# Some lo parts by ScalarE and accumulating transfers, two sorted groups of matmul passes and a sum of weights by a transfer, where the mixer's and the up projection begin

## The chip, the cores and the metric

The kernel runs on one core of a Trainium2 chip. TensorE multiplies, VectorE and ScalarE do elementwise work, GpSimd here does little but issue transfers, SyncE issues most of the loads and stores. The metric is the device time of one execution, in microseconds (us), less is better; the reference's outputs are to be met in float32.

## The reference

One step of a layer with 512 prompt tokens and 8 sampled ones, in float32: a mixer (a short gated convolution and a gated linear attention side by side), then a gated convolutional feed-forward block.

```python
def mixer(xn, conv_prev, gla_prev, w_in, conv_w, gate_w2, gate_b, gla_norm_g, w_out, chunk):
    proj = xn @ w_in
    bg, cg, hin, q, k, v, og, glr = jnp.split(proj, [_S1, _S2, _S3, _S4, _S5, _S6, _S7], axis=-1)
    cu, conv_new = causal_dwconv(cg * hin, conv_prev, conv_w)
    ya = bg * cu
    ...
    out = jnp.concatenate([ya, yb], axis=-1) @ w_out
    return out, conv_new, s_new

def conv_ffn(xn, prev, w_up, conv_w, conv_b, w_down):
    u, v = jnp.split(xn @ w_up, 2, axis=-1)
    cu, new = causal_dwconv(u, prev, conv_w)
    h = jax.nn.silu(cu + conv_b) * v
    return h @ w_down, new

    # in trunk, for the one layer
        m, c_new, s_new = mixer(rmsnorm(x, norm_mix_g[l]), conv_prev[l], gla_prev[l], w_in[l],
                                conv_w[l], gate_w2[l], gate_b[l], gla_norm_g[l], w_out[l], chunk)
        x = x + m
        f, f_new = conv_ffn(rmsnorm(x, norm_ffn_g[l]), ffn_prev[l], w_up[l], ffn_conv_w[l],
                            ffn_conv_b[l], w_down[l])
        x = x + f
```

The model width is 2048, the feed-forward width 5632, so `w_up` has 11264 columns.

## The kernel before

**Three passes.** A float32 product is made of three matmuls in a rounded format. `split` (L121) writes `hi`, a rounded copy of a tile, by ScalarE (L123), and `lo = src - hi` by VectorE (L124); a product then adds w_hi·x_hi, w_lo·x_hi and w_hi·x_lo. Activations are held transposed, 128 channels by T = 520 tokens, and a matmul takes half of them, HT = 260.

**Seven products.** The large projections are cut into groups: 12 of the mixer's ("mix"), 2 × 4 of the output projection ("wo", two halves c of the contraction by four g of the columns), 44 of the up projection ("up"), then "down". Each group is a 2 × 2 block product made with seven products instead of eight, in the order 1, 5, 6, 2, 7, 3, 4, of 24 matmuls each. It needs sums of weights (`s` and one `raw`, made by L1318 on VectorE, where the seventh product's sum `raw[2,1] + raw[1,1]` may be an accumulating transfer from GpSimd instead, L1322) and sums of activations, the forms f = 4 to 7. Forms 1, 2, 3 are the activations themselves. In the traces a tile of hi activations is called `yh`, its lo `yl`, or `bh` and `bl`, or `b` for both, where it lies in the memory of a residual tile `acc`.

**What sets the order.** The main loop runs over the products (`up_product`, `chunk_product`). While product i runs, `prepare(i + 2)` issues hi (L1373) and lo (L1377) of the weights two products ahead, and `run_steps` takes further work from generators which name the half product at which they go on. The order of the instructions on TensorE, VectorE, ScalarE and GpSimd is held as it was written; each engine works through its own queue in that order, so that a waiting instruction holds up all behind it.

**Where mix begins.** Ahead of its first group stands a projection (L140). `begin(0)` loads its weights; its seventh sum is VectorE's. `load_sum` (L1749) loads a sum of activations from DRAM into the lo tile, and returns a `split` to be called later; `put_sums` (L1851) calls those of the forms 6 and 7 while the first group runs. `R2` is the square of the normalizing factor R.

**Where up begins.** During the second half of wo (c = 1), `projected(g)` (L1682) takes each finished quarter q of the residual, `acc[g, q]`. `ready` stores it (`x_d<-acc`) and scales it into a tile `t`; `square` squares it into `fh` by ScalarE and adds that onto `ssq` or `R` by an accumulating transfer (L1706). `split` makes the forms 1, 2, 3, and `out` either splits the sums or, for g < 3, stores them in DRAM (`t_d`), to be loaded back as `yl` and split by `split_sums`; form 7 is split at once for every g. Form 2 and 3's tiles lie in the memory of `acc` tiles, so that they can be written only when the store of that quarter has read it. The first product of up waits for the last of all this, that of g = 3.

Of the kernel before, what the change touches and what calls it, by code (L numbers as in the profile page):

```python
# [9 lines left out]
F32 = mybir.dt.float32  # L10
F32R = mybir.dt.float32r
U8 = mybir.dt.uint8
AF = mybir.ActivationFunctionType
ALU = mybir.AluOpType
# [23 lines left out]
def trunk_kernel(  # L38
# [6 lines left out]
    nc = tc.nc  # L45
# [75 lines left out]
    def split(src, hi, lo, scale=None):  # L121
        if scale is None:
            nc.scalar.activation(hi, src, AF.Copy)  # L123
            nc.vector.tensor_tensor(lo, src, hi.bitcast(F32), op=ALU.subtract)  # L124
        else:
            nc.scalar.activation(hi, src, AF.Copy, scale=scale)
            nc.vector.scalar_tensor_tensor(
                lo, src, scale, hi.bitcast(F32), op0=ALU.mult, op1=ALU.subtract
            )

    def halves(t):
        return t[:, :HT], t[:, HT:T]
# [44 lines left out]
    def span(ps, w, acts, k0, pk0, nk, nkt):  # L177

        outs = [x[:, :HT] for x in ps]
        for k in range(k0, k0 + nk):  # L180
            mm3(outs, (w[0][:, k - pk0, :], w[1][:, k - pk0, :]), acts[k], k == 0, k == nkt - 1)
# [93 lines left out]
    mt_d = dp.tile([4, 4, P, T], F32, name="mt_d")  # L275
# [475 lines left out]
    xq, homes = {}, {}  # L751
# [539 lines left out]
    def source(kind, at):  # L1291
        if kind == "mix":
            return lambda m, k: mix_source(*at, m, k)
        if kind == "up":
            return lambda m, k: up_source(*at, m, k)
        return lambda m, k: chunk_source(kind, w_out if kind == "wo" else w_down, *at, m, k)
# [50 lines left out]
    def begin(n):  # L1347
        kind, at = groups[n]

        state[kind, at] = weights(  # L1350
            source(kind, at), kind == "up" or kind in ("mix", "wo") and at[0] > 0,
            None if n else early,
        )

# [32 lines left out]
    def up_product(i):  # L1387
        kind, at, r = order[i]
        st = state[kind, at]
        b = BANK[r]  # L1390
        if b not in st["bank"]:
            st["bank"][b] = mm_bank()[:, :HT]
        wh, wl = (x.rearrange("p (k c) -> p k c", k=8) for x in (his.pop(i), los.pop(i)))
        for k in range(8):
            xh, xl = xq[INPUT[r], k]
            for j, (w, x) in enumerate(((wh, xh), (wl, xh), (wh, xl))):
                nc.tensor.matmul(  # L1397
                    st["bank"][b], w[:, k, :], x, start=b not in st["used"] and k == 0 and j == 0,
                    stop=k == 7 and j == 2, skip_group_check=True,
                )  # L1400
        st["used"].add(b)

    def copied(st, b):
# [36 lines left out]
    def mult(out, x, y):  # L1440
        nc.vector.tensor_tensor(out, x, y, op=ALU.mult)
# [240 lines left out]
    def projected(g):  # L1682
# [24 lines left out]

        def out(f, t):

            if f == 7 or g == NG - 1:  # L1710
                split(t, *form(f, g))
            else:
                nc.sync.dma_start(t_d[f - 4, g], t)

# [29 lines left out]
        square(2)  # L1744
        out(6, t3)
        yield 11
        split(xg[3], *form(3, g))

    def load_sum(d, f, g):  # L1749

        hi, lo = form(f, g)
        x = lo.bitcast(F32)
        nc.sync.dma_start(x, d[f - 4, g])
        return lambda: split(x, hi, lo)

    def split_sums():
# [63 lines left out]
    ps = new_mm()  # L1820
    w = next_half()
    prepare(0)
    span(ps, w, xa, 0, 0, 4, KD)
    for x in put[:3]:
        x()
# [5 lines left out]
        x()  # L1831
    evac(ps, y9)
    mult(y8, y8, on[0])
    mult(R2, R, R)
    bctx.close()
    yt3 = yctx.enter_context(tc.tile_pool(name="yt3", bufs=1))
    slots[12:] = [yt3] * 4
    put += [load_sum(mt_d, 7, g) for g in range(4)]
    for k in range(8):
        for f, kk, b in ((1, k, 0), (2, k + 8, 0), (3, k + 8, 1)):  # L1840
            xq[f, k] = [xa[kk][x][b] for x in range(2)]
# [7 lines left out]
        yield from leave(8, y8, y9)  # L1849

    def put_sums():  # L1851
        for x, n in zip(put[6:], (1, 1.5, 2, 3.5, 4, 4.5, 5)):
            yield n
            x()

# [252 lines left out]
```

## Time and profile before

| what | before |
|---|---|
| median of three runs | 2139.94 us (2136.82 to 2142.19) |
| the profiled execution | 2138.38 us |
| its span in the profile | 2136.7 us |
| granted TensorE clock | 0.997 |
| first product of mix, of up | about 376 us, 784 us |

The profile gives each engine's busy time. A view of waits names for an engine the line that waited, and what ended the wait; a row of the timeline gives start, duration, engine, line, operation, output <- inputs, and in brackets the idle time ahead of it with its releaser. Names there have no numbers: `R2 <- R` reads `R<-R`. "DVE" is VectorE, "ACT" ScalarE, "PE" TensorE, "POOL" GpSimd, "SP" SyncE. A row of the windows view has the stretch and its length, the busy time of PE, its weight loads, DVE, ACT and POOL with their instruction counts, the granted clock, the share of the 16 DMA engines, and GB/s.

### The profile page before, as it was taken

To read this page: it belongs to the slowest core of one execution; us is meant where nothing else is said; L and a number is where in the kernel's file an instruction comes from. 1 tells how busy PE (TensorE), PEld (TensorE's weight loads), DVE (VectorE), ACT (ScalarE), POOL (GpSimd) and SP (SyncE) were. 2 spreads that over 40 slices of the span, in tenths; PEclk is the share of its full clock that TensorE was granted. 3 is DMA by queue.
4 is the path that set the end of the run, shared out by engine and by line. 5 is a ranking of instruction groups with operands and counts; after the bars stand their busy time and mean duration, and the time that the engine had idled before them with its cause. 6 is when DMAs were issued, how large, how long until landed. Compare 5 with 4: busy or idle time off the path is not lost.

```text
span 2136.7 us, 44234 instructions
## 1 busy us (share of the span) xinstructions
PE 2109.9 (99%) x17880; PEld 2088.1 (98%) x17880; DVE 1763.6 (83%) x2349; ACT 1121.8 (53%) x1688; POOL 436.0 (20%) x623
## 2 busy tenths in 40 slices
PE   9999999999999999999999999999999999999997
PEld 8999989999999989999999999999999999999997
DVE  6556675988878898988988988988989778888886
ACT  7444543545544686555555555555555554444445
POOL 4212331112234211211311221212212200300000
PEclk9999999999999999999999999999999999999999
DMA  8455646877798996776776676776766875994734
GB/s 257 131 151 171 180 127 183 222 189 205 187 286 240 268 293 157 183 186 175 181 187 172 182 187 169 181 189 167 189 182 183 292 224 150 274 293 131 222 110 159
DMA packets 467757, 417.30 MB, mean 195 GB/s; under 512 B 21769, under 2 KB 426521, under 8 KB 467409
## 3 DMA queue, kind: packets, MB, share of 16 engines
q1 hardware_dynamic: 424209, 289.84, 47.8%
q0 software_dynamic: 43296, 124.57, 22.3%
q8 instruction: 140, 2.29, 0.5%
q14 instruction: 64, 0.52, 0.1%
q10 hardware_dynamic: 48, 0.07, 0.0%
HBM read 299.65 MB, written 80.31 MB: 178 GB/s over the span
## 4 chain that ended last, share of the span: by engine, by line
PE 62%; DMA 1%; DVE 1%; issue 1%; ACT 0%; POOL 0%; ACTq 0%; DVEq 0%; SPq 0%; POOLq 0%
PE mm L1397 29%; PE ms L1397 12%; PE x L1640 7%; PE y L1640 7%; PE f L1640 3%; PE e L1640 3%; PE mm L140 2%; DMA ssq<-fh 1%; DMA x_d<-acc 0%; PE ms L1998 0%; DMA yl<-t_d 0%; DVE yl L124 0%; DVE lo L1377 0%; DVE s L1318 0%; ACT y L2061 0%
## 5 line engine op out<-in xcount | busy, mean ns | idle before, releaser
L1397 PE MATMUL mm<-yl,hi 128*128 128x260 f32 x1792 | 504.1, 281 | 2.8 <-DVE yl L124 2.8
L1397 PE MATMUL mm<-yh,hi 128*128 128x260 f32 x1792 | 502.5, 280 | 0.6 <-DVE t L701 0.6
L1397 PE MATMUL mm<-yh,lo 128*128 128x260 f32 x1792 | 502.0, 280 | 0.8 <-DVE lo L1377 0.8
L1373 ACT ACTIVATE hi<-raw 128x1024 fp32r<-128x1024 f32 x336 | 354.4, 1055 | 245.4 <-issue 89.3
L1377 DVE TENSOR_TENSOR lo<-raw,hi 128x1024 fp32r<-128x1024 f32 x336 | 410.2, 1221 | 44.6 <-ACT hi L1373 40.8
L1377 DVE TENSOR_TENSOR lo<-s,hi 128x1024 fp32r<-128x1024 f32 x252 | 309.4, 1228 | 131.3 <-ACT hi L1373 129.9
L1373 ACT ACTIVATE hi<-s 128x1024 fp32r<-128x1024 f32 x252 | 266.3, 1057 | 233.2 <-PE ms L1397 97.3
L1397 PEld LDWEIGHTS mm<-yl,hi 128*128 128x128 f32 x1792 | 336.6, 188 | 3.7 <-DVE yl L124 3.7
L1397 PEld LDWEIGHTS mm<-yh,lo 128*128 128x128 f32 x1792 | 337.8, 189 | 1.2 <-DVE lo L1377 1.2
L1397 PEld LDWEIGHTS mm<-yh,hi 128*128 128x128 f32 x1792 | 337.7, 188 | 0.8 <-issue 0.8
L1397 PE MATMUL ms<-b,hi 128*128 128x260 f32 x1408 | 264.9, 280 | 0.0
L1397 PEld LDWEIGHTS ms<-b,hi 128*128 128x128 f32 x1408 | 222.0, 188 | 0.0
L1640 PE MATMUL y<-form,hi 128*128 128x260 f32 x1120 | 211.6, 281 | 0.6 <-DVE acc L1659 0.6
L1640 PE MATMUL x<-form,hi 128*128 128x260 f32 x1120 | 211.7, 281 | 0.1
L1318 DVE TENSOR_TENSOR s<-s,raw 128x1024 f32<-128x1024 f32 x168 | 205.2, 1222 | 2.9
L1397 PE MATMUL ms<-b,lo 128*128 128x260 f32 x704 | 197.0, 280 | 0.0
L1640 PEld LDWEIGHTS y<-form,hi 128*128 128x128 f32 x1120 | 176.5, 188 | 0.9 <-ACT hi L1373 0.7
L1640 PEld LDWEIGHTS x<-form,hi 128*128 128x128 f32 x1120 | 176.5, 188 | 0.6 <-issue 0.4
L1640 PE MATMUL x<-form,lo 128*128 128x260 f32 x560 | 157.0, 280 | 0.1
L1640 PE MATMUL y<-form,lo 128*128 128x260 f32 x560 | 156.9, 280 | 0.1
L1397 PEld LDWEIGHTS ms<-b,lo 128*128 128x128 f32 x704 | 132.0, 187 | 0.0
L1397 PE MATMUL mm<-bh,hi 128*128 128x260 f32 x448 | 125.5, 280 | 1.0 <-DVE acc L1659 1.0
(402 smaller groups left out, 4847.3 us busy)
## 6 DMA issues: line engine op xcount, KB each, us to landing
raw<-in_w_up_dram SPq DMA_DIRECT2D x176, 512.0 KB, 4.7
raw<-in_w_down_dram SPq DMA_DIRECT2D x96, 512.0 KB, 7.3
raw<-in_w_in_dram SPq DMA_DIRECT2D x92, 512.0 KB, 5.0
form<-f_d SPq DMA_DIRECT2D x126, 260.0 KB, 6.0
raw<-raw POOLq DMA_DIRECT2D x59, 512.0 KB, 5.3
f_d<-t POOLq DMA_DIRECT2D x80, 260.0 KB, 5.5
raw<-in_w_out_dram SPq DMA_DIRECT2D x32, 512.0 KB, 10.8
form<-g_d POOLq DMA_DIRECT2D x42, 260.0 KB, 7.5
```

The source lines that it names most:

```text
L140: nc.tensor.matmul(o, w, xx, start=first and i == 0, stop=last and i == 2)
L1318: return lambda: nc.vector.tensor_tensor(out, x, y, op=ALU.add)
L1373: nc.scalar.activation(his[i], src, AF.Copy)
L1377: nc.vector.tensor_tensor(los[i], src, his[i].bitcast(F32), op=ALU.subtract)
L1397: nc.tensor.matmul(st["bank"][b], w[:, k, :], x, start=b not in st["used"] and k == 0 and j == 0, stop=k == 7 and j == 2, skip_group_check ...
L1640: nc.tensor.matmul(ps[:, m, :], w[:, k, m * P : (m + 1) * P], x, start=b not in st["used"] and k == 0 and j == 0, stop=k == 3 and j == 2, ...
```

## The change

1. A new `split_by_dma`: ScalarE writes hi and then lo = −hi, and GpSimd issues a transfer that adds the source onto lo in memory. VectorE has no part in it.
2. `projected(g)` uses it for g = 0, 1, 2 in place of `split` for the forms 7 and 3; g = 3 stays. `put_sums` uses it for form 7 of g = 0 and 1, where the source of the transfer is the sum in DRAM. Eight subtractions of 128x520 leave VectorE, eight copies come to ScalarE, eight transfers of 260 KB to GpSimd's queue.
3. The seventh sum of the first mix group is an accumulating transfer too, issued right after `prepare(0)`.
4. `up_product` sorts the passes of the first group of mix and of up: over all eight k, those with the weights' lo part come last in mix, those with the activations' lo part in up. In the other groups the order is the old one.
5. The square of R goes from VectorE to ScalarE, and four of the times of `put_sums` come earlier.

```diff
--- before.py
+++ after.py
@@ -127,6 +127,12 @@
             nc.vector.scalar_tensor_tensor(
                 lo, src, scale, hi.bitcast(F32), op0=ALU.mult, op1=ALU.subtract
             )
+
+    def split_by_dma(src, hi, lo, again=None):
+        nc.scalar.activation(hi, src, AF.Copy)
+        nc.scalar.activation(lo, hi.bitcast(F32), AF.Copy, scale=-1.0)
+        again = src if again is None else again
+        nc.gpsimd.dma_start(lo.bitcast(F32), again, accum_op=ALU.add)
 
     def halves(t):
         return t[:, :HT], t[:, HT:T]
@@ -1348,7 +1354,7 @@
         kind, at = groups[n]
 
         state[kind, at] = weights(
-            source(kind, at), kind == "up" or kind in ("mix", "wo") and at[0] > 0,
+            source(kind, at), kind in ("mix", "up") or kind == "wo" and at[0] > 0,
             None if n else early,
         )
 
@@ -1391,13 +1397,16 @@
         if b not in st["bank"]:
             st["bank"][b] = mm_bank()[:, :HT]
         wh, wl = (x.rearrange("p (k c) -> p k c", k=8) for x in (his.pop(i), los.pop(i)))
-        for k in range(8):
-            xh, xl = xq[INPUT[r], k]
-            for j, (w, x) in enumerate(((wh, xh), (wl, xh), (wh, xl))):
-                nc.tensor.matmul(
-                    st["bank"][b], w[:, k, :], x, start=b not in st["used"] and k == 0 and j == 0,
-                    stop=k == 7 and j == 2, skip_group_check=True,
-                )
+        passes = [(k, j) for k in range(8) for j in range(3)]
+        if at == (0,):
+            late = 2 if kind == "up" else 1
+            passes.sort(key=lambda p: p[1] == late)
+        for k, j in passes:
+            x, w = xq[INPUT[r], k][j == 2], (wh, wl, wh)[j]
+            nc.tensor.matmul(
+                st["bank"][b], w[:, k, :], x, start=b not in st["used"] and (k, j) == (0, 0),
+                stop=(k, j) == (7, 2), skip_group_check=True,
+            )
         st["used"].add(b)
 
     def copied(st, b):
@@ -1707,8 +1716,10 @@
 
         def out(f, t):
 
-            if f == 7 or g == NG - 1:
+            if g == NG - 1:
                 split(t, *form(f, g))
+            elif f == 7:
+                split_by_dma(t, *form(f, g))
             else:
                 nc.sync.dma_start(t_d[f - 4, g], t)
 
@@ -1744,13 +1755,15 @@
         square(2)
         out(6, t3)
         yield 11
-        split(xg[3], *form(3, g))
-
-    def load_sum(d, f, g):
+        (split if g == NG - 1 else split_by_dma)(xg[3], *form(3, g))
+
+    def load_sum(d, f, g, by_dma=False):
 
         hi, lo = form(f, g)
         x = lo.bitcast(F32)
         nc.sync.dma_start(x, d[f - 4, g])
+        if by_dma:
+            return lambda: split_by_dma(x, hi, lo, d[f - 4, g])
         return lambda: split(x, hi, lo)
 
     def split_sums():
@@ -1820,6 +1833,7 @@
     ps = new_mm()
     w = next_half()
     prepare(0)
+    state[groups[0]]["seventh"]()
     span(ps, w, xa, 0, 0, 4, KD)
     for x in put[:3]:
         x()
@@ -1831,11 +1845,11 @@
         x()
     evac(ps, y9)
     mult(y8, y8, on[0])
-    mult(R2, R, R)
+    nc.scalar.activation(R2, R, AF.Square)
     bctx.close()
     yt3 = yctx.enter_context(tc.tile_pool(name="yt3", bufs=1))
     slots[12:] = [yt3] * 4
-    put += [load_sum(mt_d, 7, g) for g in range(4)]
+    put += [load_sum(mt_d, 7, g, g < 2) for g in range(4)]
     for k in range(8):
         for f, kk, b in ((1, k, 0), (2, k + 8, 0), (3, k + 8, 1)):
             xq[f, k] = [xa[kk][x][b] for x in range(2)]
@@ -1849,7 +1863,7 @@
         yield from leave(8, y8, y9)
 
     def put_sums():
-        for x, n in zip(put[6:], (1, 1.5, 2, 3.5, 4, 4.5, 5)):
+        for x, n in zip(put[6:], (1, 1.5, 2, 2.5, 3, 4, 4.5)):
             yield n
             x()
 
```

In the queues this reads as follows; the line numbers are those of each kernel's own file, so that L124's subtraction and the copies keep theirs while L1377 becomes L1383. VectorE, in the second half of the first mix group, from a lo part of `s` on (`t` and `zpad` are tiles of the mixer's gate):

```order
L1377 TENSOR_TENSOR lo_4977<-s_4663,hi_4975 128x1024
L124 TENSOR_TENSOR yl12_4821<-yl12_4821,yh12_4820 128x520
L704 TENSOR_TENSOR t_5007<-zpad0_854 128x260
L698 SCALAR_TENSOR_TENSOR t_5007<-t_5007,t_4688 128x260
L704 TENSOR_TENSOR t_5008<-t_4688,zpad0_854 128x260
L698 SCALAR_TENSOR_TENSOR t_5008<-t_5007,t_4688 128x260
L124 TENSOR_TENSOR yl13_4824<-yl13_4824,yh13_4823 128x520
L1377 TENSOR_TENSOR lo_5017<-raw_4534,hi_5015 128x1024
L124 TENSOR_TENSOR zpad0_854<-zpad0_854,fh_5019 128x260
L124 TENSOR_TENSOR yl14_4827<-yl14_4827,yh14_4826 128x520
L701 TENSOR_TENSOR t_5026<-mm_4840,t_4914 128x260
L124 TENSOR_TENSOR yl15_4830<-yl15_4830,yh15_4829 128x520
```

and now:

```order
L1383 TENSOR_TENSOR lo_4983<-s_4663,hi_4981 128x1024
L710 TENSOR_TENSOR t_5011<-zpad0_854 128x260
L704 SCALAR_TENSOR_TENSOR t_5011<-t_5011,t_4688 128x260
L710 TENSOR_TENSOR t_5012<-t_4688,zpad0_854 128x260
L704 SCALAR_TENSOR_TENSOR t_5012<-t_5011,t_4688 128x260
L124 TENSOR_TENSOR yl14_4828<-yl14_4828,yh14_4827 128x520
L1383 TENSOR_TENSOR lo_5021<-raw_4534,hi_5019 128x1024
L124 TENSOR_TENSOR zpad0_854<-zpad0_854,fh_5023 128x260
L124 TENSOR_TENSOR yl15_4831<-yl15_4831,yh15_4830 128x520
L707 TENSOR_TENSOR t_5030<-mm_4841,t_4914 128x260
```

The subtractions of yl12 and yl13 are gone, yl14's moved up by two places, and yl15's stands ahead of the `t` that is read from the product's bank `mm`. Further up in the queue `R2<-R` and the sum of weights `raw<-raw,raw` are gone.

ScalarE, at the end of wo, from the last square of g = 2 to the split of the first tile of g = 3 (`b2` is form 3 of g = 2, `bh` form 1 of g = 3; DMAHW names transfers that SyncE issues, DMASW those of GpSimd):

```order
L1705 ACTIVATE fh_9812<-acc_8272 128x520 [waits DMASW7_49]
L123 ACTIVATE b2_9847<-t_9607 128x520 [waits DMAHW3_49,Activation_49]
L1373 ACTIVATE hi_9851<-raw_9383 128x1024 [waits PE_49]
L1696 ACTIVATE t_9856<-acc_8521,par_124 128x260 [waits DMAHW6_49,DVE_49]
L1696 ACTIVATE t_9856<-acc_8521,par_124 128x260
L123 ACTIVATE bh_9859<-t_9856 128x520 [waits Activation_49]
```

and now:

```order
L1714 ACTIVATE fh_9819<-acc_8274 128x520 [waits DMASW6_49]
L132 ACTIVATE b2_9854<-t_9613 128x520 [waits DMAHW3_49]
L133 ACTIVATE b2_9855<-b2_9854 128x520 [waits DMAHW7_49,Activation_49]
L1379 ACTIVATE hi_9859<-raw_9387 128x1024 [waits PE_49]
L1705 ACTIVATE t_9864<-acc_8523,par_124 128x260 [waits DMASW1_49,DVE_49]
L1705 ACTIVATE t_9864<-acc_8523,par_124 128x260
L123 ACTIVATE bh_9867<-t_9864 128x520 [waits Activation_49]
```

Behind `b2`'s hi copy stands a copy for its lo tile, and with it the wait for DMAHW7, which is the store of the residual quarter in whose memory this tile lies. In before VectorE's subtraction had that wait.

GpSimd in the same place (`R` and `ssq` take the squares, `raw` is the seventh sum of the next group's weights):

```order
L1706 DMA ssq_8898<-fh_9610 128x520
L1706 DMA R_128<-fh_9647 128x520
L1706 DMA R_128<-fh_9764 128x520
L1706 DMA ssq_8898<-fh_9812 128x520
L1322 DMA raw_9654<-raw_9651 128x1024
```

and now:

```order
L1715 DMA ssq_8900<-fh_9616 128x520
L1715 DMA R_128<-fh_9653 128x520
L1715 DMA R_128<-fh_9770 128x520
L135 DMA yl0_9774<-t_9698 128x520
L1715 DMA ssq_8900<-fh_9819 128x520
L135 DMA b2_9855<-t_9613 128x520
L1328 DMA raw_9660<-raw_9657 128x1024
```

A transfer for yl0 and one for b2 come between the squares' and ahead of the sum of weights; b2's waits for ScalarE's copy.

## The prediction

> **What bounds the kernel now.** I read the page first: how long each engine works.
>
> ```profile
> span 2136.7 us, 44234 instructions
> PE 2109.9 (99%) x17880; PEld 2088.1 (98%) x17880; DVE 1763.6 (83%) x2349; ACT 1121.8 (53%) x1688; POOL 436.0 (20%) x623
> ```
>
> TensorE stands still for 2136.7 − 2109.9 = 27 us in the whole run. The change removes no matmul, so only stalls can go, and only those at the two places it touches. Next I asked for TensorE's waits in those stretches, 376 to 400 us (first group of the mixer's projection) and 779 to 806 us (first group of the up projection).
>
> ```profile
> PE mm L1397 <- DVE lo L1377: 0.8, 2, 0.4
> PE mm L1397 <- DVE t L701: 0.6, 1, 0.6
> ...
> PE mm L1397 <- DVE yl L124: 2.8, 4, 0.8
> PE mm L1397 <- DVE acc L1659: 1.0, 1, 1.0
> PE ms L1905 <- DVE acc L1659: 0.7, 1, 0.7
> PE y L1640 <- DVE acc L1659: 0.6, 1, 0.6
> ```
>
> The columns are the total, the times, the longest. The first two rows are the mixer, 1.4 us; the other four are the up projection, 5.1 us. VectorE ends every one. The timeline of TensorE shows what a stall costs beside its wait.
>
> ```profile
> 382.29 0.28 PE L1397 MATMUL mm<-yh,hi 128*128 128x260 f32 x1
> 383.00 0.39 PE L1397 MATMUL mm<-yh,lo 128*128 128x260 f32 x1 [0.43 <-DVE lo L1377]
> ...
> 395.57 0.28 PE L1397 MATMUL ms<-xl,hi 128*128 128x260 f32 x1
> 396.49 0.36 PE L1397 MATMUL mm<-yh,hi 128*128 128x260 f32 x1 [0.64 <-DVE t L701]
> ...
> 795.74 0.39 PE L1397 MATMUL mm<-yl,hi 128*128 128x260 f32 x1 [0.77 <-DVE yl L124]
> 795.96 0.28 PE L1397 MATMUL mm<-yh,hi 128*128 128x260 f32 x1
> 796.08 0.28 PE L1397 MATMUL mm<-yh,lo 128*128 128x260 f32 x1
> 796.20 0.28 PE L1397 MATMUL mm<-yl,hi 128*128 128x260 f32 x1
> ```
>
> Undisturbed matmuls start 0.12 us apart (795.96, 796.08, 796.20). From 395.57 to 396.49 it is 0.92, so this wait of 0.64 costs 0.80: some 0.16 of refilling per stall. The mixer's three stalls then cost 1.4 + 3 × 0.16 = 1.9 us, the up projection's seven 5.1 + 7 × 0.16 = 6.2 us. **The ceiling of any gain is 8.1 us, 0.38%.** A measurement of this kernel can tell about 0.3%, 6.4 us, from no change: the change would have to take four fifths of all there is.
>
> **The mixer's part: about −1.1 us.**
>
> ```profile
> 378.20 1.06 ACT L1373 ACTIVATE hi<-s 128x1024 fp32r<-128x1024 f32 x1 [1.48 <-DVE s L1318]
> ...
> 381.12 0.69 DVE L1441 TENSOR_TENSOR R<-R 128x520 f32<-128x520 f32 x1
> 381.73 1.22 DVE L1377 TENSOR_TENSOR lo<-s,hi 128x1024 fp32r<-128x1024 f32 x1
> ...
> 384.09 1.22 DVE L1318 TENSOR_TENSOR raw<-raw 128x1024 f32<-128x1024 f32 x1
> ...
> 388.72 1.22 DVE L1377 TENSOR_TENSOR lo<-raw,hi 128x1024 fp32r<-128x1024 f32 x1
> ```
>
> Each row is start, duration, operation; back to back VectorE takes 0.61 us for 128x520 (381.12 to 381.73) and 1.14 for 128x1024 (776.94 to 778.08 in the rows on the up projection). Ahead of the lo part that ends the stall of 383.00 (381.73 + 1.22 = 382.95) the square of R goes, 0.61 us. Ahead of the one of 388.72, which ends the stall of 389.99, the sum of weights goes too, 0.61 + 1.14 = 1.75 us. Besides, sorting puts the eight passes with the weights' lo part at places 17 to 24 instead of 2, 5, ...: the first is wanted 15 × 0.12 = 1.8 us later. Either alone covers waits of 0.4, so both stalls go: 0.8 + 2 × 0.16 = −1.1 us.
>
> The stall of 396.49 I leave where it is. VectorE is relieved of yl12 and yl13 as well, but their lo halves become ScalarE copies ahead of hi parts that VectorE waits for, and yl15's subtraction now stands ahead of the `t` that TensorE waits for, where it stood behind. Its bounds are −0.8 (gone) and +0.6 (one more 128x520 in front); I take 0, since ScalarE's two copies cost about what two subtractions save. The square of R, now ScalarE's, stands right ahead of the hi part of 378.20, in the 1.48 us for which ScalarE waits there for VectorE's sum (the first row); without that cover it would cost its 0.54, a copy's time (below). The times of `put_sums` only bring the last tiles' splits forward by up to one step; no yl row of the mixer waits for its load, so 0.
>
> The sum of weights becomes an accumulating transfer that reads and writes SBUF. Its loads and its reader in the row below:
>
> ```profile
> L1373 ACT ACTIVATE hi<-raw x3: 1042/1057/1057, 371.5 to 385.4; 128x1024 fp32r<-128x1024 f32 x3
> ...
>   DMA raw<-in_w_in_dram: 5.1, 1
> ...
> raw<-raw POOLq DMA_DIRECT2D x59, 512.0 KB, 5.3
> ```
>
> The weights are awaited for 5.1 us until 371.5, the hi part of the sum is made at 385.4, and the 59 such transfers of the run land after 5.3 us in the median: 371.5 + 5.3 = 376.8, 8.6 us of cover. With yl12 and yl13 two more accumulates enter, read at a later product. I price all three at 0, at most +0.6 if the sum's stall shows.
>
> **The up projection's part: about +1.8 us.** What VectorE and ScalarE do just ahead of its first matmul:
>
> ```profile
> 775.07 0.69 DVE L1659 TENSOR_TENSOR acc<-acc,e 128x520 f32<-128x520 f32 x1
> 776.32 0.70 DVE L124 TENSOR_TENSOR b<-t,b 128x520 fp32r<-128x520 f32 x1 [0.56 <-DMA x_d<-acc]
> 776.94 1.22 DVE L1377 TENSOR_TENSOR lo<-raw,hi 128x1024 fp32r<-128x1024 f32 x1
> 778.08 0.70 DVE L124 TENSOR_TENSOR bl<-t,bh 128x520 fp32r<-128x520 f32 x1
> ...
> 786.04 0.70 DVE L124 TENSOR_TENSOR yl<-yl,yh 128x520 fp32r<-128x520 f32 x1 [0.17 <-ACT yh L123]
> ...
> 791.89 0.70 DVE L124 TENSOR_TENSOR b<-t,b 128x520 fp32r<-128x520 f32 x1 [0.23 <-DMA x_d<-acc]
> ...
> 772.59 0.62 ACT L123 ACTIVATE b<-t 128x520 fp32r<-128x520 f32 x1
> 773.28 1.06 ACT L1373 ACTIVATE hi<-raw 128x1024 fp32r<-128x1024 f32 x1
> 775.79 0.92 ACT L1696 ACTIVATE t<-acc,par 128x260 f32<-128x260 f32 x2 [1.45 <-DVE acc L1659]
> 776.75 0.64 ACT L123 ACTIVATE bh<-t 128x520 fp32r<-128x520 f32 x1
> ```
>
> The lo part `b` of 776.32 waits until a store of the residual (`x_d<-acc`) has left the tile that it overwrites. Now ScalarE writes that tile first, so **ScalarE inherits the wait**, and behind it in its queue stand the hi part of 773.28, `t` of 775.79 and `bh`. In before these were free to run; now, from 776.3: the copy 0.54 (back to back; a row's 0.64 has its end in it), hi 0.96 (to 777.8), the two halves of `t` 0.8, `bh` 0.64, which ends at 779.2. VectorE's `bl` starts there instead of at 778.08: 1.2 us late, and with it acc, yl and every row of VectorE down to 809. VectorE's two later pauses in the rows, 0.17 and 0.23, absorb 0.4. So +0.8 us; the 0.61 that VectorE saves on `b` lies in the time it now waits.
>
> Could sorting help? Here the x lo passes come last, wanted at places 17 to 24 instead of 3, 6, ..., 24: the last is wanted where it was. In the rows of 795.74 to 796.20 two tiles end the product, both late. The one of 795.74 gets 2 passes, 0.24 us, more; the one of 796.20 none, and VectorE finishes it just then:
>
> ```profile
> 794.99 1.30 DVE L124 TENSOR_TENSOR yl<-t,yh 128x520 fp32r<-128x520 f32 x2
> ```
>
> Its second ends at 796.29. A product that waits for its last tile ends no sooner however the others are sorted: I price it at 0, down to −0.24 for each of the four waits for yl, −1.0.
>
> Last, the transfers. In the stretch of wo's second half and the start of up:
>
> ```profile
> 745.00:776.00 31.00, 31.00 (x260) 30.84 (x260) 30.62 (x37) 24.53 (x38) 6.00 (x7) 1.00 1.08 277
> 776.00:810.00 34.00, 28.90 (x229) 27.47 (x229) 33.00 (x41) 25.78 (x44) 5.17 (x6) 1.00 1.12 299
> ...
> ssq<-fh POOLq DMA_DIRECT2D x6, 260.0 KB, 7.9
> ```
>
> The last columns are the clock (full), the DMA engines' share and GB/s. The engines are full (1.08, 1.12), and 260 KB at 277 GB/s is 266,240 / 277,000 = 0.96 us; an accumulate that counts reading its destination takes up to twice that, 1.9. The run's accumulates into `ssq` land after 7.9 us. Three of the six new ones are issued between 752 and 776, and whatever loads or stores lie behind them land later. Of these the store that ScalarE now waits for is the one without slack; one of the three, yl0's, is issued right ahead of its landing. I take one at the lower end, +1.0, between 0 (it falls behind the store) and 3 × 1.9 = 5.7.
>
> On this the Trainium skill speaks against the change: its page "DMA: Bandwidth & Descriptors", section "Issuing engines are not separate DMA queues", has it that transfers started by GpSimd run on the same 16 DMA engines as SyncE's and interleave with them. The shares of 1.08 and 1.12 agree that there is no free engine. The same page's section "Anatomy of one DMA — SWDGE (gpsimd) path" fits 2.0 us + bytes / 436e3, by which 260 KB would land after an estimated 2.6 us and the sum for up would be +0.8; the measured 7.9 us differ, and I go by them.
>
> **Sum.** −1.1 + 0.8 + 1.0 = +0.7 us. The profiled run's own time is 2138.38 (span 2136.7), which gives 2139.1; from the median of the three runs, 2139.94, it is 2140.6. The runs shown lie between 2136.82 and 2142.19, so neither base is better: I say 2139.8, no change.
>
> **Rivals.**
>
> *VectorE's relief carries through* (0.17). For it: VectorE is busy 30.62 of 31 us ahead of the up projection, three subtractions go there (1.8 us) and `b` of 776.32 (0.6). If the store goes out and lands that much sooner, before 774.0, ScalarE never waits, VectorE comes to up 2.4 us earlier, and the mixer gives all its 1.9: −4.3, 2134.1. Against it: TensorE is busy 31.00 of 31, so the residual cannot be complete sooner than its matmuls.
>
> *The accumulates break the chain ahead of up* (0.20, slower). The chain of waits there is led by accumulates into `ssq`, not by an engine:
>
> ```profile
> 752.68 8.41 DMA ssq<-fh
> ...
> 761.62 6.12 DMA ssq<-fh
> ```
>
> ScalarE's squares wait for their landing, and its hi parts stand behind the squares. With four more accumulates ahead of 780, at 0.96 to 1.9 us, these land 3.8 to 7.6 us later. VectorE's relief in this stage, 6 × 0.61 = 3.7, hides the first 3.7; the rest stalls TensorE. At the upper end 3.9 more, the store 5.7 late instead of 1.0: −1.1 + 0.8 + 3.9 + 1.9 to 5.7, +5.5 to +9.3, about 2146. It decides when the accumulates land over 3.7 us later than 7.9 after issue.
>
> *The change does nothing where it says* (0.03): the mixer's stalls come back with another releaser (lo parts wait for ScalarE, not for their turn) and up keeps its seven. Then 2138.4.
>
> The forecast has the remaining 0.60, from −2.3 (the mixer's 1.9, sorting's 1.0 against ScalarE's 0.8 and no accumulate: −2.1) to +4 (two accumulates at 1.9 in place of 1.0): 2136 to 2143.
>
> **Range and chances.** 2134 to 2146: it leaves out the far half of the slower rival and some of the faster. Faster by over 0.3% needs 6.4 of a ceiling of 8.1: 0.03. Slower by as much is about half of the slower rival: 0.10. Within: 0.87.
>
> **What would show it.** Mixer: no wait for `lo` in 376 to 400, one for `t` of some 0.6. Up: ScalarE waiting for `x_d<-acc` ahead of its copy of lo, VectorE's `bl` some 1 to 2 us later against TensorE's work, and TensorE's waits for acc and yl adding to 6 to 7 instead of 5.1. I am wrong if TensorE waits for yl under 1.5 us there, if ScalarE does not wait for the store, or if stalls appear in 745 to 776, where TensorE has none now.

## The result, and the profile after

The changed kernel takes 2143.86 us in the median of nine runs (2141.63 to 2147.33), the kernel before 2139.10 (2136.82 to 2142.19): a ratio of 1.0028 with a 95% interval of 1.0019 to 1.0037. That is some 6 us slower by the ratio (4.1 to 7.9) and 4.8 between the medians. The forecast was no change, with 2139.8; 2143.86 lies inside its range, but the interval of the ratio leaves no change out: it is a loss. The profiled execution took 2141.63, the shortest of the nine.

The page of the profile after, its span and the engines' busy time:

```profile
span 2139.9 us, 44256 instructions
PE 2114.5 (99%) x17880; PEld 2093.9 (98%) x17880; DVE 1757.5 (82%) x2339; ACT 1126.8 (53%) x1697; POOL 443.6 (21%) x632
```

VectorE has 6 us less to do and the kernel is slower all the same. TensorE stands still for 25 us instead of 27, but its busy time has grown by 4.6 us over the same number of matmuls: they took longer. TensorE's waits, in 376 to 400 us (one row) and in 740 to 815:

```profile
PE mm L1406 <- DVE t L707: 0.3, 1, 0.3
...
PE mm L1406 <- ACT yh L123: 2.6, 3, 1.6
PE y L1649 <- ACT hi L1379: 2.0, 1, 2.0
PE x L1649 <- DVE acc L1668: 1.0, 1, 1.0
PE y L1649 <- DVE lo L1383: 0.4, 1, 0.4
PE ms L1919 <- DVE acc L1668: 0.4, 1, 0.4
```

In the mixer the waits for lo are gone. From 740 on the total is 6.4 instead of 5.1 (another wait, of 0.8 at 735.57, is shown further down), and it lies in fewer and longer pieces: 2.0 and 1.6 us at once, where before's longest was 1.01. The windows view of the same place, cut where TensorE's clock changes (the third number from the right is the granted clock):

```profile
778.27:781.68 3.41, 1.39 (x12) 1.40 (x12) 3.16 (x5) 3.41 (x7) 0.00 (x0) 1.00 1.12 275
781.68:785.10 3.42, 3.42 (x18) 3.42 (x17) 3.42 (x5) 2.24 (x4) 1.74 (x2) 0.50 1.09 318
791.92:795.34 3.42, 1.79 (x14) 1.58 (x14) 0.68 (x2) 1.68 (x3) 0.00 (x0) 1.00 1.07 337
795.34:798.75 3.41, 2.90 (x14) 2.54 (x12) 3.38 (x5) 3.41 (x7) 0.86 (x1) 0.50 1.16 320
798.75:802.17 3.42, 3.37 (x16) 3.13 (x15) 3.42 (x5) 2.69 (x5) 0.00 (x0) 0.50 1.16 264
802.17:805.58 3.41, 3.41 (x31) 3.41 (x30) 3.41 (x6) 2.64 (x6) 0.86 (x1) 1.00 1.12 315
```

**The clock is halved for 3.41 us behind a stretch of 3.41 us in which TensorE worked 1.39 or 1.79 of it**, and once more, where the halved stretch itself had a wait (2.90). The timeline shows matmuls at half clock:

```profile
800.07 0.42 PE L1406 MATMUL ms<-b,hi 128*128 128x260 f32 x1
800.29 0.42 PE L1406 MATMUL ms<-b,lo 128*128 128x260 f32 x1
800.50 0.42 PE L1406 MATMUL ms<-b,hi 128*128 128x260 f32 x1
```

They start 0.215 us apart instead of 0.12. One such stretch does 45% less work, which is 3.41 x 0.45 = 1.5 us lost where TensorE is busy all through it; three of them lose up to 4.6 us, which is the growth of the busy time. (Far from the change each of the two profiles has one more, at 125.21 in before and at 314.06 here; they balance.) Where the two long waits come from:

```profile
772.90 0.62 ACT L132 ACTIVATE b<-t 128x520 fp32r<-128x520 f32 x1
775.76 0.64 ACT L133 ACTIVATE b<-b 128x520 fp32r<-128x520 f32 x1 [2.23 <-DMA x_d<-acc]
776.31 1.04 ACT L1379 ACTIVATE hi<-raw 128x1024 fp32r<-128x1024 f32 x1
777.25 0.90 ACT L1705 ACTIVATE t<-acc,par 128x260 f32<-128x260 f32 x2
778.18 0.64 ACT L123 ACTIVATE bh<-t 128x520 fp32r<-128x520 f32 x1
...
778.86 0.70 DVE L124 TENSOR_TENSOR bl<-t,bh 128x520 fp32r<-128x520 f32 x1 [0.25 <-ACT bh L123]
...
780.31 0.36 PE L1649 MATMUL y<-form,hi 128*128 128x260 f32 x1 [2.02 <-ACT hi L1379]
...
793.38 0.64 ACT L123 ACTIVATE b<-t 128x520 fp32r<-128x520 f32 x1 [2.07 <-DMA x_d<-acc]
794.30 0.64 ACT L123 ACTIVATE yh<-yl 128x520 fp32r<-128x520 f32 x1 [0.28 <-DMA yl<-t_d]
...
794.99 0.39 PE L1406 MATMUL mm<-yh,hi 128*128 128x260 f32 x1 [1.63 <-ACT yh L123]
```

ScalarE stands for 2.23 us for the store of the residual, as the prediction had it; the hi parts of the weights stand behind it, and TensorE waits 2.02 us for one. The times of two profiles can't be compared directly here, since the changed kernel begins wo 2.64 us sooner (616.74 against 619.38). Counted in matmuls since the first of wo, the store lets ScalarE go at the 1,305th, where it let VectorE go at the 1,304th in before (776.32). The second long wait, 1.63 us in up's third product, is of another kind: there ScalarE stands for the store of a quarter of g = 3, for which it did not stand in before, and the `yh` that TensorE waits for is made behind it.

To place the loss I take from each profile the start of the first matmul of mix, of wo, of up, and of the second of the two matmuls of L1905 (before's numbering) that stand behind up's third product. In before these three stretches last 243.02, 164.24 and 12.81 us. The table has the differences from that, the number of 3.41 us stretches at half clock from 775 to 805, and the ratio of the times with its interval. One execution scatters: the stretch ahead of mix differs by up to 2.5 us from before's. Nor is the profiled execution the middle one: those of the changed kernel and of `form3_kept` are the shortest of their kernels, those of `lo_by_act`, `mix_sort` and `mix_and_up_sort` the longest. So the stages tell where time went in one execution, and the ratio how much it is over many.

| kernel | ratio (95%) | mix | wo | up's first three | half clock |
|---|---|---|---|---|---|
| changed | 1.0028 (1.0019 to 1.0037) | −1.82 | +3.52 | +2.53 | 3 |
| mix_part | 0.9993 (0.9985 to 1.0002) | −1.84 | −0.49 | +1.91 | 1 |
| projected_part | 1.0029 (1.0017 to 1.0040) | +0.07 | +3.57 | +3.21 | 1 |
| up_sort | 0.9997 (0.9988 to 1.0006) | −0.06 | +0.48 | +0.53 | 1 |
| form3_kept | 1.0003 (0.9994 to 1.0012) | −1.42 | +1.31 | −0.55 | 0 |
| lo_by_act | 1.0008 (0.9999 to 1.0017) | +0.32 | +3.14 | −0.56 | 1 |
| form3_only | 1.0019 (1.0010 to 1.0028) | −0.42 | +4.31 | +1.85 | 2 |
| form7_only | 1.0005 (0.9995 to 1.0014) | −0.13 | +0.29 | +1.61 | 1 |
| lo_later | 1.0018 (1.0009 to 1.0027) | −0.67 | +7.52 | −1.37 | 2 |
| copies_5 | 0.9997 (0.9988 to 1.0006) | −0.05 | +1.40 | −0.32 | 0 |
| copies_9 | 1.0017 (1.0008 to 1.0026) | −0.32 | +5.33 | −1.56 | 2 |
| mix_and_up_sort | 0.9997 (0.9988 to 1.0007) | −1.15 | +0.50 | +1.54 | 1 |
| mix_sort | 1.0006 (0.9997 to 1.0015) | +1.70 | +0.31 | +0.24 | 0 |
| traffic_only | 1.0014 (1.0005 to 1.0023) | +0.05 | −1.38 | +3.51 | 2 |
| mix_late15 | 1.0004 (0.9995 to 1.0013) | −1.26 | +1.60 | +1.97 | 1 |
| filled | 1.0018 (1.0009 to 1.0027) | −1.43 | +9.54 | −0.55 | 1 |
| mix_filled | 0.9998 (0.9989 to 1.0007) | −1.75 | +0.67 | +1.41 | 0 |

### The profile page after: what moved, and what is told of

Same layout as the page of the kernel before. It is cut to its first block, busy times and chain, and to the rows that moved or that the text cites. A ratio compares the mean times of both kernels' runs of the same rounds, so it can differ in the third digit from the quotient of the medians.

```text
span 2139.9 us, 44256 instructions
## 1 busy us (share of the span) xinstructions
PE 2114.5 (99%) x17880; PEld 2093.9 (98%) x17880; DVE 1757.5 (82%) x2339; ACT 1126.8 (53%) x1697; POOL 443.6 (21%) x632
## 4 chain that ended last, share of the span: by engine, by line
PE 90%; DMA 4%; DVE 3%; ACT 2%; issue 1%; POOL 0%; SPq 0%; ACTq 0%; DVEq 0%; POOLq 0%
PE mm L1406 37%; PE ms L1406 15%; PE mm L146 13%; PE x L1649 8%; PE y L1649 7%; PE e L1649 3%; PE f L1649 3%; DMA x_d<-acc 1%; DMA form<-g_d 1%; DVE lo L1383 1%; DMA yl<-t_d 1%; PE ms L1076 1%; DMA g_d<-t 1%; DMA raw<-raw 0%; PE ms L2012 0%
## 5 line engine op out<-in xcount | busy, mean ns | idle before, releaser
L1406 PE MATMUL mm<-yh,lo 128*128 128x260 f32 x1792 | 496.9, 280 | 0.0
L1383 DVE TENSOR_TENSOR lo<-raw,hi 128x1024 fp32r<-128x1024 f32 x336 | 409.9, 1220 | 50.9 <-ACT hi L1379 46.9
L1383 DVE TENSOR_TENSOR lo<-s,hi 128x1024 fp32r<-128x1024 f32 x252 | 309.3, 1227 | 133.0 <-ACT hi L1379 133.0
L1328 POOL DMA_DIRECT2D raw<-raw x60 | 54.2, 903 | 342.6 <-DVE s L1324 308.8
```

The costliest lines, as they stand in the source:

```text
L1328: return lambda: nc.gpsimd.dma_start(out, x, accum_op=ALU.add)
L1383: nc.vector.tensor_tensor(los[i], src, his[i].bitcast(F32), op=ALU.subtract)
L1406: nc.tensor.matmul(st["bank"][b], w[:, k, :], x, start=b not in st["used"] and (k, j) == (0, 0), stop=(k, j) == (7, 2), skip_group_check=True,
```

## The experiments

**Which part costs the time: four kernels.** `mix_part` is the kernel before with the mixer's edits alone:

```diff
-            source(kind, at), kind == "up" or kind in ("mix", "wo") and at[0] > 0,
+            source(kind, at), kind in ("mix", "up") or kind == "wo" and at[0] > 0,
...
+        late = {"mix": 1}.get(kind)
+        if at == (0,) and late:
+            passes.sort(key=lambda p: p[1] == late)
...
+    state[groups[0]]["seventh"]()
...
-    mult(R2, R, R)
+    nc.scalar.activation(R2, R, AF.Square)
...
-    put += [load_sum(mt_d, 7, g) for g in range(4)]
+    put += [load_sum(mt_d, 7, g, g < 2) for g in range(4)]
...
-        for x, n in zip(put[6:], (1, 1.5, 2, 3.5, 4, 4.5, 5)):
+        for x, n in zip(put[6:], (1, 1.5, 2, 2.5, 3, 4, 4.5)):
```

> The kernel before with the mixer's edits alone (sorted passes of the first mix group, sum of weights by a transfer, yl12 and yl13 by ScalarE and transfers, R squared by ScalarE, earlier put_sums). Theory A (the loss comes from ScalarE's inherited wait for the residual's store, which makes one standstill of TensorE ahead of up so long that its clock is halved): 1.1 to 2 us faster than before, no wait of TensorE for lo in 376 to 400, clock at full around 780 to 800. Theory B (the added accumulating transfers delay loads): the mixer's three transfers have cover, the same 1 to 2 us faster. Theory C (the sorting by x lo at up is at fault): the same.

`projected_part` is the kernel before with the two edits in `projected` alone:

```diff
-            if f == 7 or g == NG - 1:
+            if g == NG - 1:
                 split(t, *form(f, g))
+            elif f == 7:
+                split_by_dma(t, *form(f, g))
...
-        split(xg[3], *form(3, g))
+        (split if g == NG - 1 else split_by_dma)(xg[3], *form(3, g))
```

> The kernel before with split_by_dma in projected alone, forms 7 and 3, no sorting. Theory A: 4 to 6 us slower than before, a standstill of TensorE of 1.5 to 2 us around 778 to 781 and the granted clock at 0.5 behind it. Theory B: 3 to 6 us slower, with yl and x_d transfers landing 2 us or more later than in before. Theory C: within 1.5 us of before, since the order of passes is the old one.

`up_sort` sorts the passes of the first up group and does nothing else:

```diff
+        late = {"up": 2}.get(kind)
+        if at == (0,) and late:
+            passes.sort(key=lambda p: p[1] == late)
```

> The kernel before with only the passes of the first up group sorted, x lo last. Theories A and B: within 1 us of before, since the last lo tile is wanted at the same place, and no standstill over 1.2 us. Theory C: 2 to 4 us slower, since the hi tiles are wanted earlier (place 2k+1 instead of 3k+1) and TensorE stands for yh over 1.5 us at once, the clock halved.

`form3_kept` is the changed kernel with form 3 split as before:

```diff
-        (split if g == NG - 1 else split_by_dma)(xg[3], *form(3, g))
+        split(xg[3], *form(3, g))
```

> The changed kernel with form 3 split by VectorE as before (form 7 still by transfers). Theory A: the inherited wait is gone, 0 to 2 us faster than before, no clock of 0.5 around 780. Theory B: three of the six transfers stay, so half the loss stays: 1.5 to 3 us slower than before. Theory C: 3 to 5 us slower than before, as the changed kernel.

The table has the answers. The mixer's edits take 1.84 us out of the mixer; the time, 0.9993, is not clear of no change. `projected`'s edits alone bring the whole loss, 1.0029. Sorting at up changes nothing (0.9997) and theory C falls. With form 3 kept as before the loss goes (1.0003), so form 3 carries most of it. Theory A laid the loss to the halved clock, and that is not all of it: `projected_part` has +3.57 in wo with no half clock there (its one stretch begins at 802). In `mix_part`, whose code at up is that of before, a stretch at half clock appears near 795 too; of the four profiles with this code at up (before, `mix_part`, `mix_sort`, `mix_late15`) two have one. So before's profile shows one of the better executions of this place.

**The wait or the transfers: five kernels.** `lo_by_act` gives ScalarE the wait without a transfer; `form3_only` and `form7_only` are `projected_part` with one of its two edits; `lo_later` moves form 3's lo copy; `traffic_only` has form 3's transfers with the wait left to VectorE.

```diff
 # lo_by_act, for g < 3
+            nc.scalar.activation(lo, hi.bitcast(F32), AF.Copy, scale=-1.0)
+            nc.vector.tensor_tensor(lo, xg[3], lo.bitcast(F32), op=ALU.add)
 # lo_later, for g < 3
+            yield 11.5
+            nc.scalar.activation(lo, hi.bitcast(F32), AF.Copy, scale=-1.0)
+            nc.gpsimd.dma_start(lo.bitcast(F32), xg[3], accum_op=ALU.add)
 # traffic_only, for g < 3
+            nc.vector.tensor_scalar(lo, hi.bitcast(F32), -1.0, None, op0=ALU.mult)
+            nc.gpsimd.dma_start(lo.bitcast(F32), xg[3], accum_op=ALU.add)
```

> The kernel before, where form 3's lo tile for g = 0, 1, 2 is first written as -hi by ScalarE and then completed by VectorE's addition: ScalarE has the wait for the store, and no transfer is added. Stage lengths are those from the first matmul of wo to the first of up, 164.24 us in before, 167.8 in the run with projected's edits alone. Theory A (ScalarE's inherited wait): 2 to 4 us longer in this stage, 3 to 6 us slower in all. Theory B (the accumulates' traffic): within 0.7 us in this stage and within 1.5 us in all.

> The kernel before with split_by_dma for form 3 alone (three transfers, ScalarE has the wait). Theory A: 2 to 4 us longer from the first matmul of wo to the first of up, as with both forms. Theory B: half of it, 1.5 to 2, since three of the six transfers are there.

> The kernel before with split_by_dma for form 7 alone (three transfers, no wait for a store). Theory A: within 0.7 us from the first matmul of wo to the first of up, no clock of 0.5 between 775 and 790. Theory B: 1.3 to 2 us longer there, ScalarE's squares waiting 2 us or more for accumulates.

> The changed kernel, but form 3's copy for lo and its transfer are issued half a product later, behind ScalarE's hi part of the weights two products ahead. Theory A: the wait then holds up only t and bh, so the stage from the first matmul of wo to the first of up is 0.5 to 2 us longer than in before instead of 3.5, and the kernel is 1.5 to 4 us faster than the changed one. Theory B: the traffic is the same, so 3 to 4 us longer in this stage and within 1 us of the changed one.

> The kernel before, where form 3's lo tile for g = 0, 1, 2 is first written as -hi by VectorE, which has the wait for the store as in before, and then completed by an accumulating transfer: the three transfers without ScalarE's wait. lo_by_act (the wait without the transfers) was 1.0008 of before, form3_only (both) 1.0019. If the two add up: 1.0011, 2.3 us, the wo stage within 1 us of before, and x_d or yl transfers landing later in up's first three products. If the wait alone counts: within 1 us of before. If the transfers alone count: 4 us slower, as form3_only.

`lo_by_act`, the waits of ScalarE and of TensorE from 740 to 815, and the windows around the long one:

```profile
ACT b L1750 <- DMA x_d<-acc: 5.5, 2, 3.4
...
PE y L1640 <- ACT hi L1373: 2.2, 1, 2.2
...
783.06:786.47 3.41, 1.25 (x11) 1.22 (x11) 3.16 (x5) 3.38 (x7) 0.00 (x0) 1.00 1.10 325
786.47:789.88 3.41, 3.41 (x18) 3.41 (x18) 3.41 (x5) 2.25 (x5) 1.74 (x2) 0.50 1.06 384
```

With no transfer added, the long wait and the half clock are there: ScalarE's copy with its wait lengthens wo by 3.14 us in this profile, some 1.4 of it by the clock, as theory A had the stage. Its 3 to 6 us in the time are not there: over all executions it is 1.7 us (−0.2 to 3.6), not clear of nothing. The eleven fall into two groups, 2138.35 to 2139.98 and 2141.47 to 2143.80, and the profile is the longest; whether the half clock parts the groups is not shown. `traffic_only`, the waits of ScalarE, VectorE and TensorE:

```profile
ACT b L123 <- DMA x_d<-acc: 2.3, 1, 2.3
...
DVE b L124 <- DMA x_d<-acc: 3.2, 1, 3.2
...
PE mm L1397 <- DVE yl L124: 3.0, 3, 1.8
PE mm L1397 <- ACT yh L123: 1.4, 1, 1.4
...
793.22:796.63 3.41, 1.48 (x8) 1.07 (x8) 3.10 (x5) 3.41 (x8) 0.79 (x1) 1.00 1.14 333
796.63:800.04 3.41, 2.69 (x12) 2.70 (x13) 3.41 (x6) 2.71 (x5) 0.07 (x1) 0.50 1.15 272
```

The transfers alone do something else: wo gets 1.38 us shorter in this execution, but the stores of the last residual quarters, for whose landing the tiles `b` of g = 3 wait, land later: one that SyncE issued at 781.27 (782.20 in before) holds VectorE until 793.50 (791.89 in before), and VectorE stands 3.2 us for it instead of 0.23. TensorE's long wait then falls into up's third product, and the clock with it. The ratios add up within their intervals of about 2 us each: the wait 1.7 us (1.0008), the transfers 3.0 (1.0014), both together 4.1 measured (1.0019). The transfers alone and both together are clear of nothing, the wait alone is not. Form 7's three transfers are unclear, 1.1 us with an interval from −1.1 to 3.0. In its profile the squares do wait for accumulates:

```profile
ACT fh L1711 <- DMA ssq<-fh: 2.8, 2, 2.4
```

wo is only 0.29 us longer. `lo_later` went against theory A: the copy now stands right ahead of `t`, the store let it go only at 779.62, and TensorE stood 5.0 us at once; wo got 7.52 longer, of which the two stretches at half clock are about 2.0, since TensorE still stood for most of the first (busy 0.29 of it). In all it is 1.0018, 2 us better than the changed kernel, with overlapping intervals.

**What a standstill costs: two doses.** The kernel before, with ScalarE's hi copy of g = 2's form 3 repeated n = 5 or 9 times more:

```diff
-        split(xg[3], *form(3, g))
+        hi, lo = form(3, g)
+        for _ in range(n + 1 if g == 2 else 1):
+            nc.scalar.activation(hi, xg[3], AF.Copy)
+        nc.vector.tensor_tensor(lo, xg[3], hi.bitcast(F32), op=ALU.subtract)
```

> The kernel before, where ScalarE repeats the hi copy of g = 2's form 3 five times more, 5 x 0.53 = 2.7 us of its time at the place where the changed kernel makes it wait; no wait for a store, no transfer. 1.45 us lie in ScalarE's wait ahead of t. If a standstill costs its length alone: 1.2 us longer from the first matmul of wo to the first of up. If a 3.41 us window with TensorE busy under some 0.55 costs a window at half clock besides: 2.5 to 3, where the profile shows a clock of 0.5 behind it.

> The same with nine copies more, 4.8 us. Length alone: 3.3 us longer in this stage. With the clock: 4.8 to 6.5, one or two windows at 0.5, since a standstill of about 4 us leaves at least one window under 0.55.

```profile
778.31:781.72 3.41, 1.90 (x16) 1.74 (x15) 3.16 (x6) 3.41 (x7) 0.00 (x0) 1.00 1.11 321
781.72:785.14 3.42, 2.42 (x20) 2.24 (x19) 3.39 (x5) 2.25 (x5) 1.74 (x2) 1.00 1.06 384
...
777.15:780.57 3.42, 0.70 (x6) 0.49 (x5) 1.93 (x2) 3.36 (x7) 0.00 (x0) 1.00 1.11 294
780.57:783.98 3.41, 1.95 (x9) 1.98 (x10) 3.40 (x5) 3.41 (x7) 0.00 (x0) 0.50 1.06 384
783.98:787.39 3.41, 3.41 (x18) 3.41 (x18) 3.38 (x5) 2.23 (x5) 1.74 (x2) 0.50 1.11 341
```

The first two rows are five copies: TensorE's longest wait is 1.5 us, it works 1.90 of 3.41 (0.56), and the clock stays; wo is 1.40 longer, about the standstill's length, and the time cannot be told from before's. The other three are nine copies: 0.70 of 3.41, then two stretches at half clock; wo is 5.33 longer where length alone gives 3.3, and the time is 1.0017. From the first dose to the second wo grows by 3.9 us, for 2.1 us more of ScalarE. Part of it comes back: up's first products are 1.56 us shorter than in before, since TensorE waits less there.

**The mixer's edits one by one: three kernels.** `mix_and_up_sort` is the changed kernel with `projected` as before, `mix_sort` sorts the first mix group and nothing else, `mix_late15` is `mix_part` with yl15's split at its old time:

```diff
-        for x, n in zip(put[6:], (1, 1.5, 2, 2.5, 3, 4, 4.5)):
+        for x, n in zip(put[6:], (1, 1.5, 2, 2.5, 3, 4, 5)):
```

> The changed kernel with projected as before: the mixer's edits and both sortings. If the edits add up: 1 to 2 us faster than before, 1.9 less from mix to wo, nothing in the wo stage, within 0.5 of before in up's first three products where no window there runs at half clock.

> The kernel before with the first mix group's passes sorted, weights' lo last, and nothing else. If sorting alone removes the waits for lo: 0.7 less from mix's first product to its third, and 0.3 to 1.2 less to wo. If it needs VectorE's relief: nothing less, lo waited for at place 17.

> The mixer's edits alone with the last split of put_sums, yl15's, at its old time behind VectorE's subtraction t, instead of ahead of it. If yl15's subtraction holds up t, the wait of 0.5 for t goes and mix to wo is 0.5 to 0.7 us shorter than with the mixer's edits alone, 1.5 to 2 us faster than before in all. If t waits for ScalarE's queue: the same as the mixer's edits alone.

`mix_sort` is the one that taught something. Its wait in the mixer, and the windows there:

```profile
PE mm L1400 <- DVE t L701: 2.4, 1, 2.4
...
396.65:400.06 3.41, 1.00 (x9) 0.95 (x9) 3.41 (x6) 0.54 (x1) 0.55 (x1) 1.00 0.43 96
400.06:403.47 3.41, 3.41 (x18) 3.41 (x17) 3.38 (x5) 1.06 (x1) 0.90 (x1) 0.50 0.75 200
```

Sorted passes take the waits for lo away, TensorE comes to this place 1.6 us sooner, counted from mix's first matmul, and stands for VectorE's `t` instead, 2.4 us in place of 0.6; the clock falls. VectorE was busy throughout (3.41 of 3.41). Without VectorE's relief the sorting makes the mixer 1.70 longer in this execution; the time, 1.0006, is not clear of no change. `mix_late15` takes the wait for `t` away, and one of 0.7 for a load of `yl` stands in its place; nothing is won (1.0004). `mix_and_up_sort` (0.9997) is `mix_part` with the same uncertainty.

**Idle matmuls against the clock: two kernels, undecided.** `filled` is the changed kernel with matmuls ahead of the long waits, `mix_filled` is `mix_part` with 5 and 5 in up's third product:

```diff
+            if i == NW + 2 and n in (8, 12):
+                if "e" not in st["bank"]:
+                    st["bank"]["e"] = mm_bank()[:, :HT]
+                for _ in range(8 if n == 8 else 4):
+                    nc.tensor.matmul(
+                        st["bank"]["e"], wh[:, 0, :], xq[INPUT[r], 0][0], start=True, stop=True,
+                        skip_group_check=True,
+                    )
...
+        if i == NW - 1:
+            x = xd[kind, c, 1][0][0]
+            for _ in range(10):
+                nc.tensor.matmul(
+                    inner(st["bank"]["c"])[:, 0, :], x[:, :P], x, start=True, stop=True,
+                    skip_group_check=True,
+                )
```

> The changed kernel with 22 idle matmuls whose result nobody reads: 10 ahead of wo's last product, 8 and 4 ahead of the tiles for which TensorE stands in up's third product. They run while TensorE would stand still, 1.2, 1.0 and 0.5 us. If it is the busy share of a 3.41 us window that halves the clock: no clock of 0.5 between 775 and 805, and 2 to 4.5 us faster than the changed kernel. If a standstill costs its length alone: the same time as the changed kernel, or up to 1 us slower.

> The mixer's edits alone with 10 such idle matmuls in up's third product, 5 ahead of each of the two tiles waited for. If the clock counts: no clock of 0.5 between 785 and 805, 1 to 3 us faster than before, up to 1.5 faster than the mixer's edits alone. If not: 0.5 to 1 us slower than the mixer's edits alone, since some of the matmuls come where nothing is waited for.

In both, bank "e" holds the first product that ScalarE has copied into it for the second sum, so these matmuls write over a part of the first up group's result, and neither kernel computes the layer. The long waits of `filled` came elsewhere than in the changed kernel, 2.99 us at 761.01 and 2.19 at 790.11, each with the clock halved behind it, so it does not tell what its matmuls saved. `mix_filled` shows no half clock from 785 to 805 (its lowest window was 0.61 busy), and 0.9998: a saving of 1.5 us in some executions cannot be told from nothing. No version here beats the kernel before beyond its interval; `mix_part` comes nearest.

## Why the prediction was wrong

**What bounds the kernel: right for a gain, empty for a loss.** The ceiling of 8.1 us held: nothing tried here won more than about 1.5 us. But it spoke only of stalls that can go. That a new standstill can cost more than its length was not asked, though the trace of before had it, once, far from the change:

```profile
124.43 0.38 PE L1143 MATMUL ms<-qb,S 128*128 128x128 f32 x1 [2.08 <-DVE S L1154]
...
121.80:125.21 3.41, 1.33 (x12) 1.14 (x11) 3.28 (x6) 1.68 (x4) 0.00 (x0) 1.00 0.27 84
125.21:128.62 3.41, 3.41 (x18) 1.95 (x17) 2.76 (x5) 0.77 (x2) 0.00 (x0) 0.50 0.56 152
```

**The mixer, −1.1: right, and small.** 1.82 to 1.84 us went, within the part's bounds. No wait of TensorE for the square of R or for the sum of weights shows, as priced. "Either alone covers waits of 0.4" was wrong: `mix_sort` shows that sorting alone moves the wait on.

**Up, +1.8: the step that failed, in both its terms.** The first, **+0.8 for ScalarE's inherited wait**, had the right mechanism and instruction. At g = 2 `bl` came behind 1,324 matmuls of wo instead of 1,318, 0.7 us of TensorE's work late, where 1.2 was worked out. But I priced it at one place; form 3 is split for g = 0, 1 and 2, and ScalarE stood at each, by the waits of the changed kernel from 725 to 815:

```profile
ACT b L133 <- DMA x_d<-acc: 6.9, 3, 2.4
```

Behind each of these waits TensorE stood as well, by the timeline 0.82, 1.03 and, as shown above, 2.02 us, where before has between 700 and 780 us a single wait, 0.55 at 779.52:

```profile
731.02 0.64 ACT L133 ACTIVATE b<-b 128x520 fp32r<-128x520 f32 x1 [2.22 <-DMA x_d<-acc]
735.57 0.36 PE L1649 MATMUL y<-form,hi 128*128 128x260 f32 x1 [0.82 <-DVE acc L1668]
...
752.46 0.64 ACT L133 ACTIVATE b<-b 128x520 fp32r<-128x520 f32 x1 [2.43 <-DMA x_d<-acc]
757.00 0.36 PE L1649 MATMUL x<-form,hi 128*128 128x260 f32 x1 [1.03 <-DVE acc L1668]
```

`lo_by_act` measures the term at 1.7 us in the time (−0.2 to 3.6), 3.14 in wo of its profile, some 1.4 of it by the clock. The second, **+1.0 for the transfers**, was mis-sized: `traffic_only` measures 3.0 (1.1 to 4.9) for form 3's three alone. I took one accumulate's time in full DMA engines; what it does in that profile is to make the stores of g = 3's quarters land later, for which tiles wait that were not in my list, and that wait is long enough to halve the clock.

**The missing term: the clock.** In the changed kernel's profile wo and up's first products lost 6.05 us. The half clock makes some 3.3 of it (the third stretch ends behind them), and TensorE's idle time there grew by 2.6, from 4.6 to 7.2 us. So in this execution the waits alone cost 2.6 where the sum had +1.8 for up, and 3.3 more came from a term that the sum put at nothing.

**Sorting at up, 0: right.** `up_sort` 0.9997, and the row that waits is still the last tile's.

**The rivals.** The slower one named the price (+5.5 to +9.3) and waits ahead of 776, which came (757.00, 1.0 us), but not the cause: it laid them to the accumulates into `ssq`, if these landed over 3.7 us later. From 745 to 810 they landed after 8.8 us in the median, in before after 8.4; and `lo_by_act`, with no transfer added, has the same wait at 762.73 (0.96 us). Squares did wait for accumulates, 2.1 us in the changed kernel, and TensorE lost 0.4 by it; form 7's three transfers, which delay them, are not clear of nothing. The faster one failed at its condition: the store held ScalarE until 775.76, not to 774, in a kernel that began wo 2.64 us sooner.

**The signs.** Of the three named, two came: stalls between 745 and 776 (1.03 and 0.39 us), and TensorE no longer waits for yl at up. It waits 2.6 us for yh, the hi parts that ScalarE makes. The third did not: ScalarE does wait for the store. One slip in the working: the forecast's ends, −2.3 and +4, are −2.1 and +3.5 by the terms that stand beside them; nothing hangs on it.

The parts' measured ratios give −1.5 for the mixer, 1.7 + 3.0 for form 3 and 1.1 for form 7: +4.3 us, against +4.1 to +7.9 measured. That agrees within their intervals of about 2 us each; how the loss divides between form 3's wait, form 3's transfers and form 7's stays open within them.

## What to carry to other kernels

An instruction that is moved to a less busy engine takes its waits along, and they hold up what stands behind it in that engine's queue: look at what the first write into a reused buffer waits for, not at which engine has idle time. Several short standstills of TensorE can be cheaper than one of the same sum; before a change that gathers waits, add up TensorE's busy time in windows of 3.4 us, and count, by what was measured here, up to 1.5 us more for each that falls under half. Free engine time bought with transfers was paid for here by the transfers behind them, with the DMA engines full.

## What the runs showed of the hardware

The clock is decided by windows of 3.41 us that run free. Between 60 and 2100 us the half-clock stretches of each profile last 3.41 or 6.83 us and begin whole multiples of 3.41 apart (781.68 and 795.34 above: 4 x 3.415). Over all 18 profiles there, of windows at full clock in which TensorE was busy for 0.50 or less, 32 of 33 were followed by half clock; between 0.50 and 0.57, 4 of 10; at 0.57 and over, none of 10,677. The Trainium skill's page "TensorE: Matmul & The Clock Gate" has such a free-running window of 3413 ns, in its section "What's actually happening", and the trace agrees. Its section "HAM oscillation — how this bites in real kernels" gives as the rule no idle gaps over about 3.4 us; here waits of 1.6 to 2.1 us were enough where they fell into one window. Where a standstill lies against the windows counts: `form3_only` has the changed kernel's wait of 2.02 us too (781.78), but across the end of a window, the one of 777.90 to 781.31 was busy for 0.54 of it, and the clock stayed full. The waits themselves differ between executions as well: with before's code at up, before and `mix_sort` have no wait for yl over 0.83 us there and no half clock, `mix_part` and `mix_late15` have one of 1.8 to 1.9 us and one stretch of it.
